# Unequal token halves of 512 and 520, branch A's gated product kept in SBUF, and later column sums in a one-core decoder layer

## The chip, the cores and the metric

The kernel runs on one core of one Trainium2 chip. The metric is the time of one execution in device microseconds (us). Work runs on five engines side by side: TensorE (PE, with its weight loads as PEld), VectorE (DVE), ScalarE (ACT), GpSimd (POOL) and SyncE (SP, which issues most of the DMAs).

## What is computed

One layer of a hybrid decoder trunk, for a prompt of 1024 tokens and 8 single-token samples, 1024 features, all in float32:

```python
xn = _rmsnorm(h, pre_g)
proj = jnp.einsum('bld,de->ble', xn, w_in)          # 1024 -> 7 * 1024
u, v, z_a, x_b, z_b, g_a, g_b = jnp.split(proj, SPLITS, axis=-1)
u = jax.nn.gelu(u)
vn = _layernorm(jax.nn.gelu(v), ln_g, ln_b)
y_a = u * _chunk_spatial_mix(vn, w_s, b_s) * jax.nn.silu(z_a)
pooled, new_pool = _pool_branch(x_b, prev_pool, pos0, w_pool, pool_scale)
y_b = pooled * jax.nn.silu(z_b)
m = (jax.nn.sigmoid(g_a) * jnp.einsum('ble,ed->bld', y_a, w_pa)
     + jax.nn.sigmoid(g_b) * jnp.einsum('ble,ed->bld', y_b, w_pb))
h = h + _rmsnorm(jnp.einsum('bld,de->ble', m, w_out), post_g)
e = jnp.einsum('blp,pd->bld', p, w_ple)
gate = jax.nn.sigmoid(jnp.einsum('bld,de->ble', _rmsnorm(h, ple_in_g), w_pg))
h = h + _rmsnorm(gate * e, ple_out_g)
```

Eleven of these products are 1024 x 1024 matrices on 1032 tokens: the seven parts of `w_in`, `w_pa`, `w_pb`, `w_out` and `w_pg`.

## The kernel before

**Tokens and halves.** Prompt and samples stand side by side as 1032 token columns (`T`). They are cut into two halves of 516 (`HT`), and a half of 516 is written by two matmuls of 258 columns (`QT`), one into each of the two 512-word banks of a PSUM buffer.

**Float32 through two parts.** Every operand is split into a high part (a rounded copy, made by ACT) and a low part (the rest, made by DVE): `split`. A product is then three: high x high, high x low, low x high. So `product` runs, for 4 blocks of 128 features, 3 pairs of parts and 2 pieces, 24 matmuls of 258 columns.

**Strassen.** A "pass" multiplies 256 output features (a pair of 128-blocks) by all tokens. `strassen` does it with seven products P1 to P7 of half-size blocks instead of eight, with sums of weights (S1 to S4) and of operands (T1 to T4):

```python
plan = (("P1", "A11", "B11", "r1"), ("P6", "S2", "T2", "r2"), ("P2", "A12", "B21", "r1"),
        ("P7", "S3", "T3", "r3"), ("P5", "S1", "T1", "r4"), ("P4", "A22", "T4", "r3"),
        ("P3", "S4", "B22", "r4"))
```

Each row is a product, its weights, its operand and its PSUM buffer. Two products on one buffer accumulate: P2 on P1, P4 on P7, P3 on P5, and the earlier one has to be read (`evacuate`) before the later one starts. P1 is copied by ACT into a slot `u`; P6 and P7 are added to it by DVE (`u`, `u7`); P2, P5, P4 and P3 give the four quarters of the output, by way of `user.direct` or `user.summed`. Only three PSUM buffers of this kind exist (`accp`), and they go round.

**Stages, in this order.** v (its first pair with eight plain products, `classical`), ga, u and za by turns, xb and zb by turns with the small pooling products (`mixes`), gb: these multiply parts of `w_in` by x, four passes each. Then pa (`Merge`) and pb (`MergeB`) multiply y_A and y_B, read back from DRAM. These 35 passes and the first v pair are of the form `Features`: weights are stationary, token columns move. The last two stages, out and gate, are of the form `Tokens`: tokens are stationary, and 512 weight columns move, so that a product is 12 matmuls of 512 columns.

**Branch A's gated product.** In the pa stage `Merge` multiplies by sigmoid(g_A) (reloaded from DRAM as `ga`) and writes the result to a DRAM tensor `m1`. In the pb stage `MergeB` reloads it (the trace calls the tile `m`) and adds branch B's product into `big`, a tile of 8 x 1032 words per partition that held x, then v and pooling scratch before.

**Column sums.** The operand sums T1 to T4 of w_out and w_pg are made ahead by `column_sums`: for each of four row blocks, two loads of 512 KB, four DVE operations, two stores. `column_steps` hangs them on steps of the v stage (w_out) and of the u and za stages (w_pg).

**Who sets the order.** The kernel hands all instructions to a `Planner`, which gives each a cost and a latest start (`late`) and makes the order of every engine from them: the operation that can start soonest goes first, and among those the one due soonest. An operation may start at most `LEAD` (14 us) before it is due, a load into a slot at most `LOAD` (17 us). The 46 slots of SBUF go round too. An operation's weights are prepared (`prepare`) 3 steps ahead and fetched 6 steps ahead. So the order in the code is a wish; products may be swapped where one isn't ready. All instructions are issued on line 287, so the trace is read by tile names: `xB11h` is the high part of B11 of x, `uw` the weights of u, `acc` and `acct` the PSUM buffers of the two forms, `accm` that of the pooling mixes.

## Time and profile before

| | |
|---|---|
| time of 3 runs, median (lowest to highest) | 1029.76 us (1029.33 to 1029.83) |
| profiled execution, its span | 1029.87 us, 1028.1 us |
| mean granted TensorE clock | 0.992 |
| HBM read, written | 116.72 MB, 51.77 MB |

The span runs from the first to the last instruction; the execution's time has 1.8 us more around it. In the rows of the profile a group shows line, engine, operation, out<-in by the program's names, partitions x elements and type, the count, then busy time, mean ns of one, and the idle time before it with what ended it. "a <- b" in the waits means that a waited for b.

### The profile page before, as it was taken

The numbers are of one execution on the slowest core, as the hardware profiler recorded it, in microseconds if no ns is written. First come the engines' busy times: TensorE is split into PE (matmuls) and PEld (weight loads), VectorE is DVE, ScalarE is ACT, GpSimd is POOL, SyncE is SP. The second block draws the span as 40 slices with busy tenths as digits, with TensorE's granted clock in tenths as the row PEclk, the third lists the DMA queues.
The fourth block names the chain that finished last, engine by engine and source line by source line (L and its number), as shares of the span: only waits on it lengthen the run. The fifth ranks groups of instructions, "written<-read, shape, count | busy, mean of one in ns | idle before, by whom it ended". The sixth has DMA issues, their size and how long they took to land. (4 is left out here: it accounts for less than half of the span.)

```text
span 1028.1 us, 18781 instructions
## 1 busy us (share of the span) xinstructions
PE 1010.2 (98%) x7556; PEld 966.9 (94%) x7556; DVE 801.7 (78%) x1239; ACT 490.1 (48%) x885; POOL 76.8 (7%) x128
## 2 busy tenths in 40 slices
PE   8999999999999999999999999999999999999996
PEld 6999999999999999999999989999999998887875
DVE  5886547987678788776777887598689898879796
ACT  7764355555434333232423333472352274778563
POOL 2200000000000000000010100000000001322122
PEclk9999998999999999999999999999999999999998
DMA  9332423722254534612304066876695572488436
GB/s 337 115 124 100 167 84 102 248 84 83 83 192 158 205 141 147 217 63 73 120 16 159 24 217 231 288 271 201 191 350 195 178 286 62 105 249 304 125 80 210
DMA packets 85108, 169.25 MB, mean 165 GB/s; under 512 B 6402, under 2 KB 46386, under 8 KB 85013
## 3 DMA queue, kind: packets, MB, share of 16 engines
q1 hardware_dynamic: 82653, 160.14, 44.6%
q0 software_dynamic: 2048, 7.37, 3.9%
q8 instruction: 59, 0.97, 0.4%
q10 hardware_dynamic: 320, 0.54, 0.2%
q14 instruction: 28, 0.23, 0.1%
HBM read 116.72 MB, written 51.77 MB: 164 GB/s over the span
## 5 line engine op out<-in xcount | busy, mean ns | idle before, releaser
L287 DVE TENSOR_TENSOR u<-acc,u 128x516 f32<-128x516 f32 x106 | 73.5, 693 | 57.6 <-PE acc L287 55.2
L287 POOL TENSOR_TENSOR rstd<-ms,mhalf 128x1 f32<-128x1 f32 (+2 forms) x45 | 41.6, 927 | 231.3 <-DVE ms L287 208.4
L287 ACT ACTIVATE u<-acc 128x516 f32<-128x516 f32 x39 | 23.4, 601 | 67.2 <-PE acc L287 63.2
L287 ACT ACTIVATE zbw<-zbs 128x512 fp32r<-128x512 f32 x16 | 9.7, 628 | 34.7 <-DVE zbs L287 31.1
L287 POOL COPY big<-xb 128x1 f32<-128x1 f32 x8 | 2.9, 367 | 291.1 <-ACT xb L287 237.6
L287 ACT ACTIVATE paw<-pas 128x512 fp32r<-128x512 f32 x16 | 9.8, 629 | 30.4 <-DVE pas L287 23.7
L287 DVE TENSOR_TENSOR big<-big 128x1032 f32<-128x1032 f32 (+3 forms) x20 | 23.7, 1222 | 0.0
L287 PE MATMUL accm<-qh,wpoolw 128*128 128x258 f32 x128 | 22.0, 285 | 1.7 <-DVE zb L287 1.7
L287 ACT ACTIVATE big<-mix 128x256 f32<-128x256 f32 x32 | 12.1, 382 | 22.1 <-PE mix L287 18.5
L287 ACT ACTIVATE junk<-h 128x512 bf16<-128x512 f32 (+1 forms) x20 | 16.3, 815 | 11.6 <-DVE h L287 9.7
L287 ACT ACTIVATE pbw<-pbs 128x512 fp32r<-128x512 f32 x16 | 9.9, 628 | 25.1 <-DVE pbs L287 23.3
L287 DVE TENSOR_TENSOR big<-mix,big 128x256 f32<-128x256 f32 x32 | 13.1, 421 | 10.1 <-ACT big L287 9.8
L287 POOL MEMSET mst<- 128x1024 f32 x1 | 1.0, 956 | 263.9 <-PE acct L287 263.9
L287 ACT ACTIVATE big<-vt 128x256 f32<-128x256 f32 x32 | 12.0, 381 | 17.6 <-PE vt L287 17.5
L287 PEld LDWEIGHTS accm<-qh,wpoolw 128*128 128x128 f32 x128 | 18.1, 189 | 2.2 <-DVE zb L287 2.1
L287 ACT ACTIVATE big<-pht,gvec 128x128 f32<-128x128 f32 x64 | 17.9, 396 | 4.2 <-PE pht L287 4.2
L287 ACT ACTIVATE zaw<-zas 128x512 fp32r<-128x512 f32 x16 | 9.9, 630 | 20.4 <-DVE zas L287 12.3
L287 DVE SCALAR_TENSOR_TENSOR zb<-accm,gvec,zb 128x516 f32<-128x516 f32 x16 | 12.0, 752 | 8.7 <-PE accm L287 8.4
L287 ACT ACTIVATE gbw<-gbs 128x512 fp32r<-128x512 f32 x16 | 9.7, 626 | 17.4 <-DVE gbs L287 13.3
L287 ACT ACTIVATE uw<-us 128x512 fp32r<-128x512 f32 x16 | 9.8, 627 | 16.3 <-DVE us L287 16.0
L287 ACT ACT_TABLE_LOAD x13 | 16.7, 1283 | 1.2 <-PEq L1651 0.8
L287 PE MATMUL mix<-wst,vh 128*128 128x256 f32 x64 | 16.3, 329 | 0.9 <-DVE big L287 0.9
(686 smaller groups left out, 3763.2 us busy)
## 6 DMA issues: line engine op xcount, KB each, us to landing
ga<-ga SPq DMA_DIRECT2D x16, 516.0 KB
gb<-gb SPq DMA_DIRECT2D x16, 516.0 KB
ya<-za SPq DMA_DIRECT2D x8, 516.0 KB
yb<-zb SPq DMA_DIRECT2D x8, 516.0 KB
m<-ga SPq DMA_DIRECT2D x8, 516.0 KB
m<-m SPq DMA_DIRECT2D x8, 516.0 KB
x<-in_x_prompt_dram SPq DMA_DIRECT2D x8, 512.0 KB
vraw<-in_w_in_dram SPq DMA_DIRECT2D x8, 512.0 KB
```

The source lines that it names most:

```text
L287: getattr(getattr(self.nc, e), method)(*args, **kwargs)
```

## The change

- The token halves are 512 and 520 (`HALF`, `WIDE`). The operands B11, B21 and T4 are narrow: one matmul of 512 columns writes a whole bank. The other four are wide: two of 260. Sums of a narrow and a wide operand take the missing 8 columns as zero, so T2's last 8 columns are those of T3, and `u` has its last 8 set to zero by POOL (`memset`).
- P4 has its own PSUM buffer r5 and stands ahead of P5; T4 is loaded and cut ahead of T1.
- `Merge` writes branch A's gated product into `big`, and `MergeB` adds to it there; `m1` is gone. Three of y_A's operands are loaded through free rows of `big` instead of slots.
- The column sums of w_out and w_pg hang on steps 8 to 46 of the u and za stages. The stores of the sums of y_A and y_B are four DMAs a block instead of two.
- `LOAD` is 14 us; a slot counts as taken by whichever of its users comes first; a memset has a cost of its own; scratch outputs of squares go to slots, and `junk` is half as wide. The prompt's tokens 512 to 515 are not loaded a second time.

```diff
-HT = T // 2
-QT = HT // 2
 HALF = 512
...
+WIDE = T - HALF
+QT = WIDE // 2
...
-    LOAD, LEAD, PATIENCE, RATE, SPARE = 17.0, 14.0, 60.0, 0.36, 3
+    LOAD, LEAD, PATIENCE, RATE, SPARE = 14.0, 14.0, 60.0, 0.36, 3
...
+        @staticmethod
+        def pieces(ps, wide):
+            if not wide:
+                return [(ps[:, 0, :HALF], slice(0, HALF))]
+            return [(ps[:, q, :QT], slice(q * QT, (q + 1) * QT)) for q in range(2)]
...
+        wide = what not in ("B11", "B21", "T4")
         for k in range(4):
-            (wh, wl), (xh, xl) = weights, operand(k)
+            (wh, wl), (xh, xl) = weights, operand.at(what, k)
             for i, (w, x) in enumerate(((wh, xh), (wh, xl), (wl, xh))):
-                for o, c in form.pieces(ps):
+                for o, c in form.pieces(ps, wide):
...
-                ("P7", "S3", "T3", "r3"), ("P5", "S1", "T1", "r4"), ("P4", "A22", "T4", "r3"),
+                ("P7", "S3", "T3", "r3"), ("P4", "A22", "T4", "r5"), ("P5", "S1", "T1", "r4"),
                 ("P3", "S4", "B22", "r4"))
...
+                both = slot("u", form.sums)
+                at["u"], at["u7"] = both[:, 0], both[:, 1]
+                if form.tail:
+                    nc.gpsimd.memset(at["u"][:, HALF:], 0.0)
+                nc.scalar.activation(out=at["u"][:, :HALF], in_=ps, func=AF.Copy)
...
             elif p == "P4":
-                user.summed(1, 0, ps, at["u"], at["u7"])
+                user.summed(1, 0, ps, at["u7"][:, :HALF])
...
+                if what == "T2":
+                    split(quarter(kk, 0), hi[:, :, :HALF], lo[:, :, :HALF])
+                    split(quarter(2 + kk, 1)[:, :, HALF:], hi[:, :, HALF:], lo[:, :, HALF:])
...
+            dma(r[:, :HALF], lo[:, :HALF])
+            dma(r[:, HALF:w], hi[:, 2 * HALF :])
+            dma(r[:, w:], lo[:, HALF:])
         spill(key + "high", b, hi)
...
+        def row(self, m, j):
+            return halves(big[:, 2 * self.pair + m, :], j)
+
         def direct(self, m, j, ps):
-            o = halves(self.out[m], j)
+            mul(self.row(m, j), ps, halves(self.out[m], j))
...
+    class MergeB(Merge):
...
+            o, row = halves(self.out[m], j), self.row(m, j)
             mul(o, ps, o)
-            self.merge(m, j)
...
+            add(row, row, o)
...
-    PARTS = ("B11", "T2", "B21", "T3", "T1", "T4", "B22")
+    PARTS = ("B11", "T2", "B21", "T3", "T4", "T1", "B22")
...
-    column_steps("wo", w_out, [(vsteps[1][5], vsteps[2][1]), (vsteps[2][2], vsteps[2][5]),
-                               (vsteps[2][6], vsteps[3][2]), (vsteps[3][3], vsteps[3][6])])
-    column_steps("wg", w_pg, [(uflow[16 + 5 * i], uflow[19 + 5 * i]) for i in range(4)])
+    for n, (key, src) in enumerate((("wo", w_out), ("wg", w_pg))):
+        column_steps(key, src, [(uflow[8 + 5 * (4 * n + i)], uflow[11 + 5 * (4 * n + i)]) for i in range(4)])
...
-    LAST = ("P1", "P6", "P7", "P5", "P4", "P3", "P2")
+    LAST = ("P1", "P6", "P7", "P4", "P5", "P3", "P2")
```

More of the change, by code (lines that the diff above doesn't have):

```diff
@@ L182, in wanted @@
                 live.append(name)
-        for name, users in self.users.items():
-            if self.tags.get(name) == "slot":
-                next(iter(users)).fresh += 1
         for op in self.ops:
             op.waits = len(op.before)
+            op.fresh = {n for n in op.names if self.tags.get(n) == "slot"}
             for o in op.before:
@@ L405, in hybrid_step, with __init__, new @@
                     "T1": (0, 1), "T2": (0, 0), "T3": (1, 1), "T4": (1, 0)}
-        def __init__(self, name, quarter=quarter, width=HT):
-            self.name, self.quarter, self.width, self.parts = name, quarter, width, {}
+        def __init__(self, name, wide=WIDE):
+            self.name, self.wide, self.parts = name, wide, {}
+        def new(self, what, kk):
+            w = HALF if what in ("B11", "B21", "T4") else self.wide
+            self.parts[what, kk] = [slot(f"{self.name}{what}{c}", (P, 2, w), F32R) for c in "hl"]
+            return self.parts[what, kk]
         def cut(self, what):
@@ L541, in quarter, with product @@
             return big[:, 4 * k : 4 * k + 4, t * P : (t + 1) * P]
-    def product(form, ps, weights, operand, first, last, again=False):
+    def product(form, ps, weights, operand, what, first, last, again=False):
         plan.apart()
+        wide = what not in ("B11", "B21", "T4")
         for k in range(4):
-            (wh, wl), (xh, xl) = weights, operand(k)
+            (wh, wl), (xh, xl) = weights, operand.at(what, k)
             for i, (w, x) in enumerate(((wh, xh), (wh, xl), (wl, xh))):
-                for o, c in form.pieces(ps):
+                for o, c in form.pieces(ps, wide):
                     nc.tensor.matmul(o, w[:, k, :], x[:, c],
@@ L627, in run @@
                     at[r] = form.new()
-                product(form, at[r], weights.ready[a], lambda k: operand.at(b, k), new, True, not new)
+                product(form, at[r], weights.ready[a], operand, b, new, True, not new)
             def run_halves(a=a, b=b, r=r):
                 for c in (slice(0, QUART), slice(QUART, HALF)):
-                    product(columns(c), at[r], weights.ready[a], lambda k: operand.at(b, k), False, True, True)
+                    product(columns(c), at[r], weights.ready[a], operand, b, False, True, True)
                     user.direct(0, 0, at[r][:, c], c)
@@ L859, in ln_stats @@
                                 op0=ALU.mult, op1=ALU.mult)
-        lnv[t] = nm, rstd([square_sum(v[:n], n, part[:n])], n)
+        vh = lnv["cut", t] = slot("vh", (P, D), F32R)
+        lnv[t] = nm, rstd([square_sum(v[:n], n, part[:n], vh)], n)
     def ln_apply(t, n=P):
@@ L1136, in loads, with summed, direct @@
             self.out = [reload(self.key, 2 * self.pair + m, self.key) for m in range(2)]
+        def row(self, m, j):
+            return halves(big[:, 2 * self.pair + m, :], j)
         def direct(self, m, j, ps):
[L1139 to L1164 removed]
+            mul(self.row(m, j), ps, halves(self.out[m], j))
+        def summed(self, m, j, ps, u, free=None):
+            free = ps if free is None else free
+            add(free, ps, u)
+            self.direct(m, j, free)
+    class MergeB(Merge):
+        def direct(self, m, j, ps):
+            o, row = halves(self.out[m], j), self.row(m, j)
+            mul(o, ps, o)
+            add(row, row, o)
     def pairs_of(c0, cls, key):
@@ L1188, in hybrid_step @@
     gbsteps = [strassen(w, xop, u) for w, u in pairs_of(GB0, Gate, "gb")]
-    yaop, ybop = stored("ya", kept["ya"], HT), stored("yb", kept["yb"], HT)
+    flat, c = big.rearrange("p b t -> p (b t)"), [T + 4 * w for w in (0, HALF, HALF + WIDE, HALF + 2 * WIDE)]
+    through = {what: flat[:, c[i] : c[i + 1]] for i, what in enumerate(("T4", "T1", "B22"))}
+    yaop, ybop = stored("ya", kept["ya"], WIDE, through), stored("yb", kept["yb"], WIDE)
     merged = lambda src, i: src[:, 2 * i * P : (2 * i + 2) * P]
@@ L1466, in hybrid_step @@
     l, c = pbsteps[3], outsteps[0]
-    turn_over(woop, l, [*l[2:], c[0], c[1]], ("B11", "T3", "T2", "B21", "T1", "T4", "B22"))
+    turn_over(woop, l, [*l[2:], c[0], c[1]], ("B11", "T3", "T2", "B21", "T4", "T1", "B22"))
     l, c = outsteps[3], gatesteps[0]
```

220 lines of the change are left out of this document (101 added, 119 removed).

## The prediction

> **What bounds the kernel now.** I read the page first, then the busy time by stage, then the timeline of TensorE alone, then the waits.
>
> ```profile
> span 1028.1 us, 18781 instructions
> PE 1010.2 (98%) x7556; PEld 966.9 (94%) x7556; DVE 801.7 (78%) x1239; ACT 490.1 (48%) x885; POOL 76.8 (7%) x128
> ...
> PE   8999999999999999999999999999999999999996
> ...
> PEclk9999998999999999999999999999999999999998
> ```
>
> ```profile
> 237.00:400.00 163.00, 163.00 (x1357) 162.97 (x1356) 125.50 (x193) 71.58 (x111) 0.55 (x1) 1.00 0.44 153
> 690.00:840.00 150.00, 148.96 (x1229) 148.23 (x1229) 128.07 (x184) 57.37 (x80) 0.00 (x0) 1.00 0.68 237
> 840.00:930.00 90.00, 90.00 (x415) 73.28 (x414) 76.12 (x119) 61.37 (x135) 20.15 (x23) 1.00 0.52 151
> ```
>
> TensorE is busy in every slice, and from 237 to 400 us (u and za) for all of 163.00 us; the columns after the length are PE, PEld, DVE, ACT, POOL, granted clock, DMA share and GB/s. The chain that ended last covers only the last 2 us and says nothing of the middle. So a stage lasts as long as its matmuls take from start to start, plus the few waits. "Busy" is not yet "at its peak", hence the cost of one matmul has to come from starts.
>
> ```profile
> 363.07 0.41 PE L287 MATMUL acc<-xB11h,uw 128*128 128x258 f32 x2
> ...
> 383.33 0.40 PE L287 MATMUL acc<-xB11h,zaw 128*128 128x258 f32 x2
> ...
> 839.22 0.39 PE L287 MATMUL acct<-woB11h,mw 128*128 128x512 f32 x1
> ...
> 858.73 0.39 PE L287 MATMUL acct<-woB11h,mw 128*128 128x512 f32 x1
> ```
>
> ```profile
> 363.07:383.33 20.26, 20.26 (x170) 20.26 (x169) 18.39 (x27) 7.77 (x11) 0.00 (x0) 1.00 0.30 112
> 839.22:858.73 19.51, 19.51 (x86) 15.78 (x85) 19.25 (x26) 11.64 (x20) 0.96 (x1) 1.00 0.18 70
> ```
>
> Here is one whole Strassen pass of each form, from its first product to the first of the next (the count of a window takes in two matmuls that reach over its edge). A feature pass is 7 products of 24 matmuls of 258 columns: 20.26 us / 168 = 120.6 ns each. A token pass is 7 products of 12 matmuls of 512: 19.51 us / 84 = 232.3 ns. Two matmuls of 258 cost 241.2 ns, one of 512 costs 232.3. The slope between the two sizes is (232.3 - 120.6) / 254 = 0.44 ns a column, so about 7 ns of a matmul do not depend on its width.
>
> **The change, part by part.**
>
> *Merged matmuls.* A feature pass keeps four wide products (24 matmuls, now of 260 columns) and has three narrow ones (B11, B21, T4) of 12 matmuls of 512. There are 35 such passes (3 for v, 4 each for ga, u, za, xb, zb, gb, pa, pb). That merges 35 x 36 = 1260 pairs; the first v pair, which takes eight plain products, merges 4 x 12 = 48 and the four pooling mixes another 48. 1356 pairs x 8.9 ns = 12.1 us less. The wide ones, 35 x 96 + 96 + 96 = 3552, each get two columns more: 0.88 ns, 3.1 us more. No row shows 260 columns; nothing below the 258 row is likely, and twice the slope would be 6.2 us, so the bounds are 0 and 6.2, and I take 3.1, the 258 row being two columns away. **Net -9.0 us**, all of it on the engine that sets the end. The form 128x512 into these accumulators is what the token passes run already.
>
> The Trainium skill speaks against this size: "TensorE: Matmul & The Clock Gate", section "Wait — 56ns, not 53.3ns?", gives a warm matmul as columns over 2.4 GHz plus a fixed 2.5 ns or so. By that, an estimate, a merged pair would save 4.2 ns, a wide matmul would cost 0.83 ns more, and the sum would be -2.7 us. The two passes above differ from it: they leave about 7 ns that are fixed and 0.44 ns a column, and I go by them.
>
> *The accumulator of P4, and the order P4, P5, P3.* P4 now has its own PSUM buffer and no longer waits for P7's evacuation. But P3 accumulates on P5's buffer and now follows it directly, and P5 has to be read first. What stands in between is up to the planner, which on TensorE takes whatever can start soonest: the next pass's P1, whose operands are cut and whose weights are prepared three steps ahead. It does this already where something is late:
>
> ```profile
> 692.84 0.28 PE L287 MATMUL acc<-yaB11h,paw 128*128 128x258 f32 x1
> ...
> 695.74 0.41 PE L287 MATMUL acc<-yaB22h,paw 128*128 128x258 f32 x2
> ```
>
> There the next pass's B11 ran before this pass's B22. With P1 (2.8 us) in the gap, the evacuation is covered:
>
> ```profile
> L287 DVE TENSOR_TENSOR u<-acc,u 128x516 f32<-128x516 f32 x106 | 73.5, 693 | 57.6 <-PE acc L287 55.2
> L287 POOL MEMSET mask<- 128x8 f32 x4 | 0.4, 103 | 0.0
> L287 DVE TENSOR_TENSOR big<-pxe,gvec 128x16 f32<-128x16 f32 x4 | 0.6, 164 | 0.0
> L287 ACT ACTIVATE sst<-smixs 128x64 fp32r<-128x64 f32 x1 | 0.3, 257 | 0.0
> ```
>
> I cost it at 0. Without that cover it is the price of a rival below. P6 of the next pass then waits for P4's buffer, three products old, P4 for P6's buffer, two products old: no tighter than now, where P4 waits for P7's reading with one product between.
>
> *Small instructions.* 35 memsets of 128x8 on POOL (0.10 us each, 3.6 us on an engine that is 7% busy). Behind each stands the addition of P6, one product or 2.9 us later; a memset queued behind one of POOL's own waits would delay it, and with it P4's buffer. The tail of T2 adds 4 ACT and 4 DVE operations (0.26 and 0.16 us), and four DVE ones of that size go from the start. Scratch in a slot instead of `junk` changes no duration. All 0, in idle time of DVE (78% busy) and ACT (48%).
>
> *Branch A's product stays in `big`.* The multiplications and additions on DVE are as many as before; what goes is DMA.
>
> ```profile
> L287 SPq DMA_DIRECT2D m<-ga x8: 319/381/743, 701.2 to 784.1; - x8
> L287 SPq DMA_DIRECT2D m<-m x8: 382/418/3173, 757.9 to 821.3; - x8
> ```
>
> 16 transfers of 516 KB, 8.3 MB of the 150 us x 237 GB/s = 35.6 MB moved from 690 to 840 us, and the 3.2 us for which SP stood in one reload (the three numbers are ns: least, median, most). That stage has a TensorE wait that ends with a late weight (total us, times, longest):
>
> ```profile
> PE accm L287 <- DVE zb L287: 1.7, 2, 1.4
> PE acct L287 <- ACT ge L287: 1.0, 2, 0.5
> PE mix L287 <- DVE big L287: 0.9, 1, 0.9
> PE acc L287 <- ACT pbw L287: 0.9, 1, 0.9
> PE acct L287 <- DVE ms L287: 0.5, 1, 0.5
> ...
> ACT pbw L287 <- DMA pbraw<-in_w_pb_dram: 2.5, 1, 2.5
> ```
>
> `pbraw` landed late, then ACT, then TensorE. Against it stands the lead of loads, cut from 17 to 14 us. I take **-1.0 us** (bounds: -2 if a second short wait goes too, 0 if the shorter lead gives it back). Sixteen more store DMAs, eight of them 8 columns wide, go out where the sums of ya and yb are stored; they are read back only in the pa and pb stages.
>
> *Column sums made later.* Sixteen additions of 0.69 us for each of w_out and w_pg, 11.0 us of DVE, and their 8 loads and 8 stores of 512 KB each. Those of w_out leave the v and ga stages for u and za, those of w_pg move 12 steps back. From 237 to 400 us DVE is busy for 125.50 of 163.00; with 11 more it is at 84%. Cost 0 while DVE keeps the rest; if it did not, an evacuation late by an operation shows as a TensorE wait of about 0.7 us.
>
> *Stalls that are re-dealt.* The planner makes a new order, so every one-off stall is drawn again. The largest is here:
>
> ```profile
> 163.81 0.60 ACT L287 ACTIVATE u<-acc 128x516 f32<-128x516 f32 x1 [3.89 <-PE smix L287]
> ...
> 165.71 0.58 PE L287 MATMUL mix<-wst,vh 128*128 128x256 f32 x1 [0.88 <-DVE big L287]
> ...
> 166.63 0.52 PE L287 MATMUL acc<-xT2h,gaw 128*128 128x258 f32 x1
> ...
> 171.90 0.38 PE L287 MATMUL mix<-wst,vh 128*128 128x256 f32 x1
> ```
>
> ACT sat until `smix` was done (a slot that changed hands), the mix waited for it 0.9 us, and just then the granted clock fell: the T2 product took 5.27 us where 2.89 is usual. About 4 us in all with the slow mixes around it. It may stay or go; the sum holds it as it is (bounds -4 and 0).
>
> *The end.* The last pass now runs P4, P5, P3 and P2 in two halves. Its last half waits today for ACT:
>
> ```profile
> 1018.44 0.28 PE L287 MATMUL acct<-wgB21h,hw 128*128 128x256 f32 x1
> 1018.76 0.38 ACT L287 ACTIVATE ge<-acct 128x256 f32<-128x256 f32 x1 [0.41 <-PE acct L287]
> 1019.19 0.39 PE L287 MATMUL acct<-wgB21h,hw 128*128 128x256 f32 x1 [0.47 <-ACT ge L287]
> ```
>
> With P5's reading outstanding, P2's first half can go before P3 and P3 between the halves: the 0.6 us go, and P3's longer chain (add, sigmoid, two multiplications, square) ends about as much nearer to the end. 0, between -0.6 and +1.5.
>
> **Sum**: -9.0 - 1.0 = -10.0 us. The profiled execution took 1029.87 us (span 1028.1 and 1.8 around it), 0.1 over the median 1029.76 of the runs, so **1019.8 us**.
>
> **The rivals.**
>
> *P3 waits for P5 (slower).* If the planner leaves P3 right behind P5, TensorE idles while DVE reads P5. The rows of the end give the price of such a hand-over: 0.75 us between two matmul starts where 0.12 is usual, for an evacuation of 0.38; with 0.69 it is 0.63 + 0.31 = 0.94 us. 43 passes x 0.94 = 40 us, hence 1029.87 - 10.0 + 40.4 = 1060. It decides from 11 uncovered passes on, where 10.3 us eat the gain. For it: the order in the code itself has nothing between them. Against it: the swap in the pa stage, and the few waits of TensorE that the present order leaves. Chance 0.07.
>
> *The new order has more waits (no difference).* The waits listed above come to 5 us and the slow clock to 2.4 more; another order could double or triple them, above all where DVE is nearly full (19.25 of 19.51 us in the token pass above), and 8 to 12 us more give 1028 to 1032. For it: DVE's work stays while TensorE's shrinks. Against it: the one buffer shared with a single product between now occurs once in a pass, not twice, and the pb stage gets DMA to spare. Chance 0.08.
>
> *Half the merge's worth.* The token pass may owe its speed to its stage: PEld is busy 73.28 of 90.00 us there and 162.97 of 163.00 in u and za. If only half of the 8.9 ns came from merging, -6.0 + 3.1 - 1.0 gives 1026. The page's rule named above would land close to this, with its 2.5 ns fixed. Against it: both kinds of pass are at full clock, without waits, and with a weight load for every matmul. Chance 0.07. That the change doesn't do what it says is part of it: narrow products that stay in two pieces would show as 128x256 forms.
>
> *The stall at 164 us and the slow clock go too.* Another slot for `u` and no w_out sums on DVE near there: -4 more, 1016, and down to 1013 if the waits of the mixes and the gate go as well. Chance 0.28.
>
> **How the numbers follow.** The forecast, 1017 to 1025, has 0.50; the stall's end 0.28; half the worth 0.07; no difference 0.08; slower 0.07. The first three are faster by over 0.2% (2.1 us, about what a measurement of this kernel can tell from no change): 0.85. Same 0.08, slower 0.07. The range 1013 to 1026.5 leaves out the last two cases and a little of the rest; it takes in 6.2 instead of 3.1 us for the 260 columns.
>
> **What would show it.** Some 6200 matmuls instead of 7556. A feature pass from B11 to B11 of 20.02 us, narrow products of 2.79 and wide ones of 2.92. On TensorE the next pass's B11 between T1 and B22, and no wait `acc <- DVE` there. No `m` among the DMA issues, and no `pbw` wait on DMA. Wrong would be: a matmul of 260 columns above 123 ns, one of 512 above 236 ns in u and za, waits of over 10 us in all behind P5, or a second stretch of reduced clock.

## The result, and the profile after

| | before | after |
|---|---|---|
| time, median (lowest to highest) | 1029.8 us (1029.33 to 1030.72, 6 runs) | 1005.7 us (1005.36 to 1006.97, 6 runs) |
| ratio to before, 95% interval | | 0.9768 [0.9755, 0.9781] |
| profiled execution, its span | 1029.87 us, 1028.1 us | 1006.03 us, 1003.7 us |
| mean granted TensorE clock | 0.992 | 0.998 |

The kernel became 24 us faster. The forecast was 10 us, 1019.8, and its range ended at 1013: the direction was right, the size wrong by more than a factor of two. (Of before_fresh, below, one execution, the profiled one, took 1985 us; the figures for that kernel are of its other nine.)

The page of the changed kernel, its first lines and the clock:

```profile
span 1003.7 us, 16146 instructions
PE 987.7 (98%) x6200; PEld 887.4 (88%) x6200; DVE 798.0 (80%) x1237; ACT 488.1 (49%) x887; POOL 78.1 (8%) x162
...
PEclk9999999999999999999999999999999999999999
```

TensorE still sets the end, with 6200 matmuls in place of 7556, exactly the 1356 merged pairs. The stretch of reduced clock near 165 us isn't there in this execution.

One feature pass, B11 of u to B11 of za, in the timeline of TensorE (first rows of its products) and as a window (length, then PE, PEld, DVE, ACT, POOL, clock, DMA share, GB/s):

```profile
309.17 0.40 PE L289 MATMUL acc<-xB11h,uw 128*128 128x512 f32 x1
...
311.95 0.40 PE L289 MATMUL acc<-xB22h,zaw 128*128 128x260 f32 x2
...
314.83 0.40 PE L289 MATMUL acc<-xT2h,uw 128*128 128x260 f32 x2
...
326.11 0.40 PE L289 MATMUL acc<-xT1h,uw 128*128 128x260 f32 x2
...
328.99 0.39 PE L289 MATMUL acc<-xB11h,zaw 128*128 128x512 f32 x1
```

```profile
309.17:328.99 19.82, 19.82 (x135) 18.24 (x133) 17.28 (x24) 7.76 (x11) 0.10 (x1) 1.00 0.61 230
```

A narrow product takes 311.95 - 309.17 = 2.78 us, as forecast (2.79), and a wide one 314.83 - 311.95 = 2.88, where 2.92 was forecast and a product of 258 columns took 2.89. The pass is 19.82 us (forecast 20.02). At both ends B11 of the next pass stands between T1 and B22, where the forecast put it.

The waits of TensorE in the changed kernel (total us, times, longest), all of them:

```profile
PE warm L289 <- POOL ident masks.py:199: 1.9, 1, 1.9
PE acct L289 <- DVE ms L289: 1.6, 1, 1.6
PE acct L289 <- DVE hw L289: 1.2, 1, 1.2
PE e L289 <- ACT wehi L289: 1.2, 1, 1.2
PE e L289 <- DVE welo L289: 0.8, 1, 0.8
PE pst L289 <- DVE x L289: 0.2, 1, 0.2
PE smix L289 <- DVE sv L289: 0.2, 1, 0.2
```

In the stages from ga to pb no wait is left but one of 0.2 us: `accm`, `mix` and `pbw` of the list before are gone.

**Where the 24.4 us of span went.** Two sums over all matmul starts (own reckoning from the traces): the time from a product's first matmul to the next product's, as a median by kind; and the lost time, all by which a step from one start to the next exceeds its usual length (the median of its shape) by over 40 ns, which holds waits and reduced clock alike.

| term | forecast, us | measured, us |
|---|---|---|
| 113 narrow products, 2.895 to 2.781 us each | -12.1 | -12.9 |
| 148 wide products, 2.895 to 2.875 us each | +3.1 | -3.0 |
| lost time of TensorE, 23.2 to 14.2 | -1.0 | -9.0 |
| from the last matmul to the end, 7.9 to 9.2 | 0 | +1.3 |
| sum | -10.0 | -23.6 |

The remaining 0.8 us wasn't split up. Of the 23.2 us lost before, 4.4 lie in steps at reduced clock (1.6 in the start, 2.8 in ga); in the profiled execution of the changed kernel none do. Such a stretch isn't in every execution: with those of the trace the mean granted clock is 0.992, and in single executions of the kernel before it goes from 0.992 to 0.998. The 7 of 76 at 0.997 or 0.998 took 1029.5 us in the mean, the 30 at 0.993 took 1030.5. So the trace puts 4.4 us into these stretches, while the times show about 1.

### The profile page after: what moved, and what is told of

Its sections match the earlier page's. It is cut to its first block, busy times and chain, and to the rows that moved or that the text cites. A ratio compares the mean times of both kernels' runs of the same rounds, so it can differ in the third digit from the quotient of the medians.

```text
span 1003.7 us, 16146 instructions
## 1 busy us (share of the span) xinstructions
PE 987.7 (98%) x6200; PEld 887.4 (88%) x6200; DVE 798.0 (80%) x1237; ACT 488.1 (49%) x887; POOL 78.1 (8%) x162
## 5 line engine op out<-in xcount | busy, mean ns | idle before, releaser
L289 DVE TENSOR_TENSOR u<-acc,u 128x520 f32<-128x520 f32 (+1 forms) x90 | 62.5, 695 | 38.7 <-PE acc L289 34.0
L289 POOL TENSOR_TENSOR rstd<-ms,mhalf 128x1 f32<-128x1 f32 (+1 forms) x45 | 41.6, 927 | 213.8 <-DVE ms L289 191.5
L289 ACT ACTIVATE u<-acc 128x512 f32<-128x512 f32 x39 | 23.2, 595 | 36.2 <-PE acc L289 35.9
L289 DVE TENSOR_TENSOR big<-big 128x1024 f32<-128x1024 f32 (+4 forms) x20 | 23.6, 1216 | 0.0
L289 DVE TENSOR_TENSOR xb<-acc,u 128x520 f32<-128x520 f32 (+1 forms) x12 | 8.3, 694 | 19.1 <-PE acc L289 19.1
L289 PE MATMUL accm<-qh,wpoolw 128*128 128x260 f32 (+1 forms) x96 | 20.9, 319 | 0.0
L289 ACT ACTIVATE big<-mix 128x256 f32<-128x256 f32 x32 | 12.1, 383 | 17.5 <-PE mix L289 16.9
L289 DVE TENSOR_TENSOR v<-acc,u 128x520 f32<-128x520 f32 (+1 forms) x9 | 6.3, 697 | 14.9 <-PE acc L289 14.8
L289 DVE TENSOR_TENSOR acc<-acc,u 128x512 f32<-128x512 f32 (+1 forms) x16 | 11.1, 696 | 8.7 <-PE acc L289 8.7
L289 DVE SCALAR_TENSOR_TENSOR zb<-accm,gvec,zb 128x512 f32<-128x512 f32 (+1 forms) x16 | 12.0, 751 | 6.6 <-PE accm L289 6.5
L289 ACT ACTIVATE xbw<-xbs 128x512 fp32r<-128x512 f32 x16 | 9.8, 624 | 14.7 <-DVE xbs L289 12.2
```

What stands on the lines that cost most here:

```text
L289: getattr(getattr(self.nc, e), method)(*args, **kwargs)
```

## The experiments

Two things are to be explained: why wide matmuls of *more* columns became cheaper, and what took 9 us of lost time away. Each median below is to be held against the kernel before as it was measured beside it (1029.8 to 1030.5 us), which the ratio does.

| kernel | median, us | ratio to before [95%] |
|---|---|---|
| pieces_256_260 | 1020.8 | 0.9909 [0.9895, 0.9924] |
| narrow_in_two | 1016.7 | 0.9870 [0.9855, 0.9884] |
| shift2 | 1029.4 | 0.9991 [0.9982, 1.0000] |
| shift4 | 1017.9 | 0.9877 [0.9861, 0.9893] |
| m1_in_dram | 1016.6 | 0.9877 [0.9858, 0.9896] |
| old_sums | 1010.0 | 0.9804 [0.9789, 0.9820] |
| load17 | 1011.4 | 0.9817 [0.9802, 0.9833] |
| load12 | 1008.9 | 0.9791 [0.9777, 0.9806] |
| old_fresh | 1012.0 | 0.9828 [0.9809, 0.9847] |
| p5_p4_p3 | 1005.5 | 0.9761 [0.9744, 0.9779] |
| last_old | 1006.7 | 0.9768 [0.9753, 0.9782] |
| before_m1_in_big | 1028.3 | 0.9982 [0.9972, 0.9992] |
| before_sums_late | 1030.9 | 1.0007 [0.9998, 1.0017] |
| before_p4_buffer | 1046.2 | 1.0158 [1.0141, 1.0175] |
| before_fresh | 1028.6 | 0.9986 [0.9977, 0.9996] |
| before_planner | 1037.0 | 1.0066 [1.0051, 1.0081] |
| before_planner_m1 | 1030.3 | 1.0006 [0.9996, 1.0016] |
| before_planner_m1_sums | 1028.9 | 0.9992 [0.9982, 1.0001] |

A name with `before_`, and pieces_256_260, is the kernel before with an edit; the others are the changed kernel with an edit.

### What a matmul costs: width, merging, or where its operand starts

Theory: the second of two pieces of 258 columns starts 258 x 4 = 1032 bytes into a row, 8 bytes past a multiple of 16, and that costs. Rival: the gain is the merging itself, with a fixed cost of some 7 ns for each matmul.

**pieces_256_260**: the kernel before, with pieces of 256 and 260 columns in place of 258 and 258. As many matmuls and columns; the second piece starts at byte 1024.

```diff
-        pieces = staticmethod(lambda ps: [(ps[:, q, :QT], slice(q * QT, (q + 1) * QT)) for q in range(2)])
+        pieces = staticmethod(lambda ps: [(ps[:, 0, QUART:], slice(0, QUART)),
+                                          (ps[:, 1, : HT - QUART], slice(QUART, HT))])
```

> The kernel before, with halves of 516 kept, but each half written by matmuls of 256 and 260 columns instead of 258 and 258, side by side across the border of the two banks. The columns are as many, the matmuls as many, the order of work the same; only the second piece now starts 1024 bytes into its row instead of 1032. Theory 'place' (a moving operand that does not start on a multiple of 16 bytes costs some 3.5 ns more per matmul: in the trace of before the first piece takes 118.7 ns and the second 122.3, after the change 119.5 and 119.9): a feature product falls from 2.895 to about 2.85 us, 261 of them give -11.5 us, so about 1018. Theory 'width' (258 columns are slow as such, or the feature stage was slow from waits): no change beyond 3 us, 1027 to 1033. If the second piece is slow only because a new weight load follows it, its time stays near 122 ns and nothing changes.

**narrow_in_two**: the changed kernel, with each narrow product as two matmuls of 256 columns.

```diff
-                return [(ps[:, 0, :HALF], slice(0, HALF))]
+                return [(ps[:, q, :QUART], slice(q * QUART, (q + 1) * QUART)) for q in range(2)]
```

> The changed kernel with one part undone: the narrow products go as two matmuls of 256 columns, one into each bank, instead of one of 512; 1356 matmuls are added back and nothing else. The prediction's sizing (about 7 ns of a matmul do not depend on its width): 1356 x 7 = 9.6 us more, about 1015. The other sizing (aligned pieces take 118.7 ns at 258 and 231.8 at 512 columns, so about 4 ns are fixed): 5.6 us more, about 1011. A theory by which merging is worth nothing here, since the weight loads are hidden: 1006.

**shift2 and shift4**: the changed kernel with every operand that is cut into parts moved by 2 or by 4 words (8 or 16 bytes) within a slot that is longer for it; 45 slots in place of 46.

```diff
-            self.parts[what, kk] = [slot(f"{self.name}{what}{c}", (P, 2, w), F32R) for c in "hl"]
+            pair = [slot(f"{self.name}{what}{c}", (P, 1044), F32R) for c in "hl"]
+            self.parts[what, kk] = [t[:, 2 : 2 + 2 * w].rearrange("p (k t) -> p k t", k=2) for t in pair]
```

> The changed kernel with every high and low part of the strassen operands moved by 2 words (8 bytes) inside its slot, and 45 slots instead of 46 to make room. Theory 'place': both pieces of a wide product and the one piece of a narrow product of x, ya and yb (also wo and wg) now start at 8 bytes past a multiple of 16: wide matmuls go from about 119.7 to 123 ns, 3360 x 3.5 = 11.8 us more than shift4, and up to 6 us more if matmuls of 512 columns suffer as well. Theory 'width': the same as shift4 within 1.5 us.

> The control for shift2: the same layout and 45 slots, the parts moved by 4 words (16 bytes). Theory 'place' with a grain of 16 bytes: pieces as after the change, 119.5 to 120 ns, and a time of 1005.7 give or take 3 for the order that one slot less brings. If the grain is 32 bytes or more, the pieces of this kernel are slower than those of the changed kernel.

One pass of u each, as a window, in the order pieces_256_260, narrow_in_two, shift2, shift4:

```profile
359.65:379.62 19.97, 19.97 (x170) 19.97 (x169) 18.31 (x27) 7.76 (x11) 0.00 (x0) 1.00 0.31 112
```

```profile
354.30:374.28 19.98, 19.98 (x170) 19.98 (x169) 18.40 (x26) 8.59 (x13) 0.00 (x0) 1.00 0.40 142
```

```profile
334.43:354.57 20.14, 20.14 (x135) 18.52 (x133) 15.35 (x26) 9.32 (x14) 0.10 (x1) 1.00 0.64 232
```

```profile
330.99:350.85 19.86, 19.86 (x135) 18.27 (x134) 15.12 (x26) 9.31 (x14) 0.10 (x1) 1.00 0.66 237
```

The lengths are what counts. 20.26 us before falls to 19.97 with the same 168 matmuls and as many columns: the second piece starts elsewhere, and with it the cut between the pieces and the place of the first in PSUM have moved. shift2 and shift4 differ in the start alone, by 8 bytes: with the same 132 matmuls 19.86 rises to 20.14. The mean of a matmul, start to start, by piece (own reckoning from the traces; products with a step over 135 ns, or 245 ns at 512 columns, are left out):

```
kernel           columns  second piece or operand starts  ns of the matmul
before           258      first piece, byte 0             118.7
before           258      second, byte 1032               122.3
pieces_256_260   256      first, byte 0                   118.0
pieces_256_260   260      second, byte 1024               119.9
after            260      first, byte 0; second, 1040     119.6; 119.9
after            512      byte 0                          231.4
narrow_in_two    256      first, byte 0; second, 1024     117.9; 117.6
shift4           260; 512 16 bytes on                     119.9, 119.8; 231.8
shift2           260; 512 8 bytes on                      121.8, 122.3; 233.4
```

On an aligned start all sizes lie on one line: (231.4 - 117.75) / 256 = 0.444 ns a column and about 4 ns that are fixed. Eight bytes past a multiple of 16 cost 1.6 to 3.5 ns more. That a piece is the second of its pair is not the reason: where both start on a multiple of 16, in the changed kernel and in narrow_in_two, they differ by 0.3 ns. So a merged pair saves 235.5 - 231.4 = 4.1 ns by itself, over 1356 pairs 5.6 us. The second pieces' 3.5 ns, in these pairs and in the 1776 pairs of wide matmuls, are 10.9 us; the columns (four fewer a narrow pair, four more a wide one) come to +0.8. Together -15.7, the measured -15.9. The theory holds and the rival gets a third: **two thirds of the matmul gain are the 16-byte start, one third is the merging.** The times agree: pieces_256_260 gains 9.4 us over the kernel before as measured beside it, where its piece times give 9.6 (11.5 were expected); shift2 is 11.5 us behind shift4 by the medians and 8.4 by the profiled executions, where the piece times give 10.8. narrow_in_two is 11.0 us behind the changed kernel, of which 5.6 are the pairs and the other half lost time that the order brings (19.8 us in all, 14.2 in the changed kernel). Its time alone, 1016.7, would fit the 7 ns of the prediction (1015 expected) better than the 4 ns (1011); the lengths of its matmuls decide. In pieces_256_260 the lost time stays at 24.0 us, though every product became shorter. shift4 was expected within 3 us of the changed kernel and is 12 behind, with 6.7 us more lost time in the xb and zb stages. The one slot less, in this kernel with longer slots for the parts, is the likely price; the two weren't separated.

### Who took the lost time away: parts undone

Theory: the in-SBUF product, the later sums and the planner's edits each free slots or DMA, and each carries a share. Rivals: P4's buffer and the order P4 before P5, or mere luck of a new order. The lost time by stage (us, own reckoning from starts):

```
                        start    v    ga  u/za xb/zb   gb    pa    pb  gate   all
before                    6.7  2.0   5.2   0.4   0.4  3.1   0.0   1.9   2.9  23.2
after                     5.8  1.7   1.6   0.3   0.3  0.1   0.0   0.0   3.8  14.2
m1_in_dram                5.7  1.7   1.6   0.3   0.3  0.1   0.0  11.0   3.8  25.1
old_sums                  5.3  1.7   4.2   0.3   0.3  0.1   0.0   0.0   3.8  16.3
load17                    5.7  1.7   1.7   0.3   1.6  1.2   0.0   0.4   5.2  18.4
load12                    5.5  1.7   1.8   0.6   1.3  0.1   1.2   0.1   4.4  17.1
old_fresh                 5.5  1.7   1.5   3.1   0.9  2.7   0.0   0.0   3.3  19.2
p5_p4_p3                  5.7  2.0   1.2   0.3   0.4  0.0   0.0   0.2   4.9  15.3
last_old                  7.2  1.7   1.6   0.3   0.3  0.1   0.0   0.0   4.5  16.3
```

**m1_in_dram**: the changed kernel, `Merge` writes to DRAM and `MergeB` reloads, as before.

```diff
         def direct(self, m, j, ps):
-            mul(self.row(m, j), ps, halves(self.out[m], j))
+            o = halves(self.out[m], j)
+            mul(o, ps, o)
+        def store(self):
+            for m, t in enumerate(self.out):
+                spill("m1", 2 * self.pair + m, t)
...
+            self.others = [reload("m1", 2 * self.pair + m, "m1") for m in range(2)]
...
-            add(row, row, o)
+            add(self.row(m, j), o, halves(self.others[m], j))
```

> The changed kernel with branch A's gated product written to DRAM and reloaded again (8.3 MB of DMA, 16 slots' worth of reloads back). Theory 'DMA' of the prediction: the pb stage waits for late weights again, 1 to 2 us, about 1007. Rival: the waits in pb belonged to the old order or the old buffers, and nothing changes (1006).

TensorE's wait in it, then DVE's timeline around that place, and windows of it:

```profile
PE acc L289 <- DVE ybT4l L289: 6.8, 1, 6.8
```

```profile
747.58 0.68 DVE L289 TENSOR_TENSOR big<-gb,m 128x512 f32<-128x512 f32 x1
...
752.76 1.22 DVE L289 TENSOR_TENSOR ybT4l<-ybT,ybT4h 128x1024 fp32r<-128x1024 f32 x1 [4.50 <-DMA m<-ga]
```

```profile
745.00:750.00 5.00, 2.27 (x13) 1.62 (x11) 3.26 (x6) 0.20 (x1) 0.00 (x0) 1.00 1.03 415
750.00:755.00 5.00, 0.96 (x2) 0.83 (x3) 2.24 (x2) 1.67 (x3) 0.00 (x0) 0.75 0.14 55
755.00:760.00 5.00, 5.00 (x24) 4.65 (x23) 4.71 (x6) 0.63 (x1) 0.10 (x1) 0.57 0.00 0
```

The low part of T4 needed a slot that a store of `m1` (`m<-ga`) still read, while the DMA engines were full (share 1.03). DVE stood 4.50 us for it, TensorE 6.8 us behind it, and the matmuls after that ran at a clock of 0.57. So the product in SBUF is worth 10.8 us here, by way of a slot that a transfer holds. One or two had been expected.

**old_sums**: the column sums at their old places.

```diff
-    for n, (key, src) in enumerate((("wo", w_out), ("wg", w_pg))):
-        column_steps(key, src, [(uflow[8 + 5 * (4 * n + i)], uflow[11 + 5 * (4 * n + i)]) for i in range(4)])
+    column_steps("wo", w_out, [(vsteps[1][5], vsteps[2][1]), (vsteps[2][2], vsteps[2][5]),
+                               (vsteps[2][6], vsteps[3][2]), (vsteps[3][3], vsteps[3][6])])
+    column_steps("wg", w_pg, [(uflow[16 + 5 * i], uflow[19 + 5 * i]) for i in range(4)])
```

> The changed kernel with the column sums of w_out and w_pg back on their old steps in the v, ga and u stages. Theory 'sums': DVE's 11 us in v and ga are what made the ga stage wait; 3 to 4 us come back there, about 1009, and the granted clock may drop near 165 us again. Rival 'slots': the ga stall was a slot that changed hands; then ga stays near 1.6 us of gaps and the time near 1006.

The time is 4.2 us longer. Two waits come back in the ga stage, whose lost time rises from 1.6 to 4.2 us, all of it without reduced clock; 0.6 us more pass behind the last matmul. That is what the profiled execution shows, which is 3.0 us slower than that of the changed kernel.

```profile
PE mix L289 <- DVE big L289: 1.2, 1, 1.2
...
PE acc L289 <- ACT gaw L289: 0.7, 1, 0.7
```

**load17 and load12**: the first number of `SPARE = 14.0, 14.0, ...`, the lead of loads `LOAD`, is 17 or 12.

> The changed kernel with loads allowed 17 us ahead of their due time again instead of 14. If the shorter lead frees slots that the ga and gb stages need, gaps come back there: 1008 to 1010. If the lead only moves loads, 1006, within 2 us. If 14 is too short somewhere (the prediction counted that as a possible loss), it is faster: 1003 to 1005.

> The changed kernel with loads allowed only 12 us ahead instead of 14. 17 had cost 5.7 us by slots that were taken too early (waits in xb/zb, gb and gate). If fewer slots held is still worth something: 1003 to 1005, in the gate stage, where 3.7 us of gaps are left. If 12 is too short for a load of 512 KB, weights come late: 1007 or more, with waits that end with a DMA.

14 us is the best of the three, by 5.7 and 3.2 us. With 17 lost time comes back in xb and zb, gb and gate, but not in ga, where it had been expected too; with 12 it is in xb and zb, pa and gate, and none of TensorE's waits there ends with a DMA.

**old_fresh**: a slot counts as taken by its first user in the code's order, as before, not by whichever comes first.

```diff
-            op.fresh = {n for n in op.names if self.tags.get(n) == "slot"}
+        for name, users in self.users.items():
+            if self.tags.get(name) == "slot":
+                next(iter(users)).fresh += 1
...
-            for name in list(o.fresh):
-                for user in self.users[name]:
-                    user.fresh.discard(name)
```

> The changed kernel with the old accounting of slots (the first user in the code counts). Matmuls as in the changed kernel. Theory (the accounting is what took the waits of ga and gb away): 2 to 6 us of waits come back, gb among them with 1 to 3, time 1008 to 1012. Rival (it hardly matters): within 1 us of the changed kernel's 1005.7.

6.3 us are lost, 2.8 of them in u and za, 2.6 in gb, where waits of the pooling mixes are there again:

```profile
PE accm L288 <- DVE zb L288: 0.8, 2, 0.4
PE accm L288 <- ACT wpoolw L288: 0.8, 1, 0.8
```

**p5_p4_p3 and last_old**: the old order P5, P4, P3 everywhere, P4 keeping r5 (in the pa and pb stages P5's sum then overwrites the values to which P4 is added, so one quarter of those products is computed from another value); and the old order in the last pass alone.

```diff
-                ("P7", "S3", "T3", "r3"), ("P4", "A22", "T4", "r5"), ("P5", "S1", "T1", "r4"),
+                ("P7", "S3", "T3", "r3"), ("P5", "S1", "T1", "r4"), ("P4", "A22", "T4", "r5"),
...
```

```diff
-    LAST = ("P1", "P6", "P7", "P4", "P5", "P3", "P2")
+    LAST = ("P1", "P6", "P7", "P5", "P4", "P3", "P2")
```

> The changed kernel with one thing undone: the products stand in the old order P5, P4, P3 again (T1 loaded and cut before T4), with P4's own buffer kept. Theory 'order': the waits that went from TensorE (9 us less in gaps: 3.6 in ga, 3.0 at the last pooling mixes in gb, 1.9 in pb) went because P4 is early and only P5 to P3 is tight, a place the next pass fills; then some 3 to 6 us of gaps come back, 1009 to 1012. Theory 'the buffer alone': 1006, gaps as in the changed kernel. The rival of the prediction, by which P5 right before P3 costs: this kernel is faster than the changed one.

> The changed kernel with the last pass of the gate stage alone back in the order P5, P4, P3, P2. With P3 behind P5 the last pass ends in P2, P3, P2, and the time from the last matmul to the end is 9.2 us where it was 7.9 before. Expected: the end falls by 1.2 us, TensorE waits 0.6 us between P2's halves as before, in all 0.5 to 1 us less than the changed kernel: about 1005.

Neither moves the time by more than 1 us, so in the changed kernel the order of the products is out as a rival. P4's own buffer stays in both runs: what it does in the changed kernel wasn't tried. last_old had been expected 0.5 to 1 us faster and is 1 us slower; its profiled execution has a stretch of half clock in the start (10.7 to 14.1 us), that of the changed kernel none.

Undone one at a time, the in-SBUF product, the later sums, the shorter lead and the accounting of slots cost 10.8, 4.2, 5.7 and 6.3 us. That is 27 us, where 9.0 us of lost time went in all: the parts hang on each other.

### The parts alone, in the kernel before

If each part had its own worth, it would show in the kernel before as well.

**before_m1_in_big** has the in-SBUF product alone, **before_sums_late** the later sums alone (the diff of old_sums turned round).

```diff
         def direct(self, m, j, ps):
-            o = halves(self.out[m], j)
-            mul(o, ps, o)
-            self.merge(m, j)
+            mul(self.row(m, j), ps, halves(self.out[m], j))
```

> The kernel before with one part of the change alone: branch A's gated product stays in the tile big, no writes to m1 and no reloads of it. The changed kernel without this part was 10.8 us slower, all of it in the pb stage, where a slot was held by a write to m1. Theory 'slots and queue': in the kernel before, the only waits of the pb stage are 1.9 us of gaps; these go, so 1028, and no more. Theory 'worth by itself': about 10 us less, 1020.

> The kernel before with the later column sums alone. In the changed kernel the old place cost 2.9 us in the ga stage (gaps 1.6 to 4.2). Theory 'sums': ga loses some 3 us, and with the wait the stretch of half clock at 165 us (2.4 us) may go as well: 1025 to 1027. Rival 'slots': the new order brings other waits and the time stays within 2 us of 1029.8.

The first gains 1.75 us, as the theory of slots had it. The second gains nothing that can be told, and its trace keeps the stretch of half clock at 165 us. What was worth 10.8 and 4.2 us in the changed kernel is worth next to nothing in the old one.

**before_p4_buffer** has P4's buffer and the order P4, P5, P3 alone.

```diff
-                ("P7", "S3", "T3", "r3"), ("P5", "S1", "T1", "r4"), ("P4", "A22", "T4", "r3"),
+                ("P7", "S3", "T3", "r3"), ("P4", "A22", "T4", "r5"), ("P5", "S1", "T1", "r4"),
```

> The kernel before with one edit of the change alone: P4 gets a PSUM buffer of its own, r5, and stands ahead of P5, T4 ahead of T1; the pieces stay 258 wide, all else as before. Its matmuls are as many and as wide, so a pass keeps its 20.26 us. Theory (the third buffer's turn is what held the pooling mixes of the gb stage): TensorE's idle time in gb falls from 3.1 us to under 0.5 and the time to about 1027, ratio 0.997. Rival (those waits hang on slots and on when loads start, as one slot less and the 17 us lead each brought 1.2 us of them back): gb keeps about 3 us, time 1029 to 1031, ratio 1.000. A third case: P4 and P5 both outstanding ahead of P3 adds waits elsewhere, over 1032.

It is 16 us slower, beyond the 1032 of the third case. TensorE's lost time in ga is 15.8 us in place of 5.2; some 5 us more are lost in the gate stage, and the end is 1.3 us longer. The two longest waits of TensorE, both in ga, then DVE's timeline in that stage, and windows of it:

```profile
PE acc L287 <- ACT gaw L287: 2.9, 1, 2.9
PE mix L287 <- DVE vl L287: 2.6, 1, 2.6
```

```profile
188.03 0.69 DVE L287 TENSOR_TENSOR woraw<-woraw,woraw 128x512 f32<-128x512 f32 x1 [0.30 <-DMA woraw<-in_w_out_dram]
188.76 0.69 DVE L287 TENSOR_TENSOR woraw<-woraw 128x512 f32<-128x512 f32 x1
189.49 1.42 DVE L287 TENSOR_TENSOR woraw<-woraw,woraw 128x512 f32<-128x512 f32 x2
190.82 1.22 DVE L287 TENSOR_TENSOR vl<-big,vh 128x1024 fp32r<-128x1024 f32 x1
```

```profile
190.00:192.00 2.00, 0.00 (x0) 0.00 (x0) 1.97 (x3) 0.49 (x2) 0.00 (x0) 0.87 1.10 392
192.00:194.00 2.00, 1.91 (x9) 1.91 (x10) 1.83 (x5) 0.56 (x2) 0.00 (x0) 0.50 1.02 405
194.00:196.00 2.00, 2.00 (x11) 2.00 (x11) 0.52 (x1) 0.00 (x0) 0.00 (x0) 0.50 1.03 420
```

DVE makes four additions of the column sums of w_out, 2.8 us, ahead of `vl`, the low part of v, for which TensorE waits 2.56 us (to 192.09); then the clock is at half until 198. The wait for the weights `gaw` ends at 202.62, again with additions of these sums on DVE ahead of it, and the clock is at half until 208.6. Whether later sums would have ended these two waits wasn't tried; the two that old_sums brings back in ga are likewise a mix's for DVE and a product's for `gaw`. In gb 2.1 of the 3.1 us stay. The waits are not at P3 behind P5, of which the third case spoke.

**before_fresh** has the new accounting of slots alone, **before_planner** that and the lead of 14 us; **before_planner_m1** adds the in-SBUF product, **before_planner_m1_sums** the later sums too. All four keep the 7556 matmuls. (The diffs are those of old_fresh, load17, m1_in_dram and old_sums turned round.)

> The kernel before with the planner's new accounting of slots alone (a slot counts as taken by whichever of its users comes first). Matmuls as before, so stages keep their length but for waits. Theory (the accounting sets when slots change hands, and the pooling mixes of gb wait for slots): the 3.1 us of waits in gb fall under 0.5 and the 5.2 of ga by a microsecond or more, time 1023 to 1027. Rival (the accounting re-deals waits but takes none away; the sum of all parts is needed): 1028 to 1034, waits of 20 us or more in all.

> The kernel before with the new accounting of slots and the lead of loads of 14 instead of 17 us. Theory (the planner's edits carry the 9 us of waits that went, since the 17 us in the changed kernel brought 4.2 us of waits back): waits 14 to 18 us in all, time 1019 to 1025. Rival (they need the slots that m1's removal and the later sums set free): waits stay above 20 us, time 1027 to 1034.

> The kernel before with the planner's edits (accounting of slots, lead of loads 14 us) and with branch A's gated product kept in SBUF, nothing else: as many matmuls of 258 columns as before. Theory (the planner's edits take the waits of gb and part of those of ga away, and the reloads and stores of m1 are what made them cost 5.7 us in pa and 6.9 in pb): gb stays under 0.5 us of waits, ga near 3, pa and pb fall back to under 1 each, all waits 15 to 19 us, time 1021 to 1026. Rival (the waits of pa and pb come from the shorter lead itself): pa and pb keep 8 us or more, time 1032 to 1038. A third case: gains that do not add, 1027 to 1031.

> The same with the later column sums as well. Theory (the sums made later free slots and DVE in ga, worth 4.2 us in the changed kernel): ga falls from about 3 to under 2 us of waits, time 1 to 3 us under the run without them, 1019 to 1024. Rival (the parts re-deal waits, and their sum is not to be had from a list): no better than the run without them, or worse.

```
                        start    v    ga  u/za xb/zb   gb    pa    pb  gate   all
before                    6.7  2.0   5.2   0.4   0.4  3.1   0.0   1.9   2.9  23.2
before_planner            6.7  2.0   3.2   0.3   0.4  0.0   5.7   6.9   4.4  30.1
before_planner_m1         6.8  2.0   3.2   0.3   0.4  0.0   5.7   0.0   4.3  23.3
before_planner_m1_sums    6.7  2.0   1.2   0.3   0.4  0.0   6.5   0.0   4.4  22.1
```

(before_fresh gains 1.5 us by its times and isn't in this table.) Here most parts take away one thing, and put another in its place. The planner's edits end the waits of gb, and bring 5.7 us into pa and 6.9 into pb; the kernel is 7 us slower. The in-SBUF product ends those of pb and leaves those of pa as they are. The later sums make the kernel 1.4 us faster by the medians. In ga the column shows mostly the clock (own reckoning): 2.8 us at reduced clock in the kernel before, 1.5 in before_planner and before_planner_m1, none in before_planner_m1_sums; the waits there are 1.0, 0.5, 0.6 and 0.0 us. The waits of before_planner, and of before_planner_m1:

```profile
PE acc L288 <- DVE ybT4l L288: 3.2, 1, 3.2
PE acc L288 <- DVE yaB22l L288: 2.4, 1, 2.4
...
PE acc L288 <- DVE paw L288: 1.2, 1, 1.2
...
PE acc L288 <- DVE pbw L288: 1.1, 1, 1.1
```

```profile
PE acc L288 <- DVE yaB22l L288: 2.4, 1, 2.4
...
PE acc L288 <- DVE paw L288: 1.2, 1, 1.2
```

So both theories of before_planner_m1 were half right: pb's waits were those of `m1`, pa's were not. What is left in pa is the low part of y_A's B22, cut too late. DVE's and TensorE's timelines of before_planner_m1, then of the changed kernel:

```profile
687.77 0.40 PE L288 MATMUL acc<-yaB22h,paw 128*128 128x258 f32 x2
689.32 2.37 DVE L288 TENSOR_TENSOR yaB22l<-yaB,yaB22h 128x1032 fp32r<-128x1032 f32 x2
690.60 0.51 PE L288 MATMUL acc<-yaB22l,paw 128*128 128x258 f32 x2 [2.42 <-DVE yaB22l L288]
```

```profile
665.90 1.23 DVE L289 TENSOR_TENSOR yaB22l<-big,yaB22h 128x1040 fp32r<-128x1040 f32 x1
...
668.26 1.23 DVE L289 TENSOR_TENSOR yaB22l<-big,yaB22h 128x1040 fp32r<-128x1040 f32 x1
...
674.21 0.40 PE L289 MATMUL acc<-yaB22h,paw 128*128 128x260 f32 x2
```

The first matmul of pa stands at 670.45 in the one and at 651.65 in the other. From there on the two cuts start after 18.9 us in before_planner_m1, and after 14.3 and 16.6 in the changed kernel. The product that needs them starts after 17.3 and after 22.6 us, because in the changed kernel gb's last product and the next pass's B11 run ahead of it. So two things differ: the cut is earlier, from a row of `big` in place of a slot (the three operands of y_A that are loaded through free rows), and the product is later. Which of the two empties pa wasn't tried, nor were P4's buffer in the changed kernel and the scratch outputs in slots undone by themselves.

## Why the prediction was wrong, point by point

- **What bounds the kernel.** Right. TensorE sets the end before and after, and a stage lasts as long as its matmuls and waits: every gain above is one or the other.
- **Merged matmuls, 12.1 us.** The size came out (12.9), the reason did not. "So about 7 ns of a matmul do not depend on its width" is the step that failed: the 120.6 ns of that pass are the mean of 118.8 for first and 122.4 for second pieces, and the second holds the price of a start 8 bytes past a multiple of 16. The size came out all the same, because it was the difference of two measured rows, whatever made it. The fixed part is 4 ns, and merging alone gives 4.1 ns a pair. The rival "half the merge's worth" had that right and was still further off in time, since it kept the +3.1. The Trainium skill's rule, "TensorE: Matmul & The Clock Gate", section "Wait — 56ns, not 53.3ns?", with 2.5 ns fixed, is nearer to these 4 ns than the 7 were; its 0.417 ns a column (an estimate from its 2.4 GHz) is not what these traces show, 0.444.
- **Wide matmuls.** "The wide ones, 35 x 96 + 96 + 96 = 3552, each get two columns more: 0.88 ns, 3.1 us more": the term with the wrong sign, -3.0 us. "Nothing below the 258 row is likely" closed the range on the side where the answer lay. Halves of 520 make the second piece start at byte 1040, a multiple of 16. What was overlooked was to be seen in the trace of before: with the products' matmuls set apart by piece, first and second differ by 3.5 ns.
- **The order P4, P5, P3.** Right: the next pass's P1 fills the gap, and with the old order, P4 keeping its buffer, the time is the same to 0.2 us. The rival in which P3 waits for P5 (1060) did not come. That buffer and order alone cost 16 us in the kernel before was not foreseen; most of it is in ga.
- **Branch A's product in `big`, -1.0 us.** Mis-sized. In the finished kernel pb lost 1.9 us of waits, the upper bound; but without it the changed kernel is 10.8 us slower, since the other edits put 11 us of lost time into pb that this one takes out. Its worth was reckoned in bytes moved; what TensorE waited for was a slot that such a transfer held.
- **Column sums later, 0.** Mis-sized: 4.2 us in the changed kernel, of which 2.6 are lost time in ga. Cost was weighed where the sums go; the gain lies where they left. In the kernel before the same edit gains nothing.
- **Stalls that are re-dealt, 0 (-4 to 0).** This term failed: but for branch A's 1.0 us the lost time was held as it was, and it fell by 9.0. The rival with 0.28 came nearer, but stopped at 1013: ga -3.6, gb -3.0, pb -1.9 and start -0.9 us, against gate +0.9. In gb and pb it was no lottery: the planner's edits and the in-SBUF product switch these waits on and off, in both kernels. In ga the later sums do so plainly in the changed kernel alone; 2.8 of the 3.6 us there, and all that the start gained, are stretches of reduced clock, which come in one execution and not in the next.
- **The end, 0 (-0.6 to +1.5).** +1.3, within its bounds; with the old order in the last pass it is 8.0 us again, and the kernel is no faster: in that trace start and gate lose 2.1 us more, the start by its stretch of half clock.

The steps that failed, then, are these two. A matmul's cost was taken to hang on its width alone, with one price for both pieces and 7 ns of it fixed; that left out what the second piece's start costs, and gave the wide term the wrong sign (6.1 us). And the lost time was held as it was (8 us, waits and reduced clock together).

## What to carry to other kernels

Before a cost is split into a fixed and a width part, set the matmuls apart by where their operand starts; a piece length that is a multiple of 4 words made each second piece about 3.5 ns cheaper than its width lets expect, at no other price that these runs show. In a kernel whose order a planner makes from a scarce pool of slots, the worth of a part can't be read from the kernel before: the same edit gave 1.7 us there and 10.8 in company, and P4's buffer with the new order cost 16 us alone, while going back to the old order in company changed nothing. So ask of each edit which slots, and until when, it holds, and try the parts undone from the end as well as done from the start.

## What the runs showed of the hardware

A moving operand in the fp32r form that starts 8 bytes past a multiple of 16 costs a matmul of 260 columns 1.9 to 2.5 ns (shift2 against shift4), one of 512 columns 1.6 ns; a second piece of 258 columns costs 3.5 ns more than the first (kernel before). How it is at 4 bytes wasn't measured.

After the longer waits of TensorE the granted clock was 0.50, in stretches of 3.4 or 6.8 us that reached 3 to 7 us beyond the wait: in before_p4_buffer after 2.56 us (the windows above), in load17 after 2.61, in before_planner_m1_sums after 2.42, in m1_in_dram after 6.8. Such a wait costs its length and about half of the time behind it again: the 6.8 and 0.9 us of waits in pb of m1_in_dram became 11.0 us of lost time. A wait of 2.19 us in the gate stage of before_p4_buffer left the clock at 1.00. The Trainium skill, "TensorE: Matmul & The Clock Gate", section "What's actually happening", has the clock halved after an idle window of about 3.4 us; the half clock is what these traces show, but 2.42 to 2.61 us without work were enough.

Length alone does not decide it. In the ga stage 16 matmuls of 8x8 take 1.9 us (`smix`), and in 8 of the 19 traces, the one of before among them, the clock fell 2 to 5 us after they began; in the other 11, with the same 16 matmuls, it did not. In before_planner it fell with no wait ahead of it. TensorE's timeline there, and windows of it:

```profile
161.78 1.95 PE L288 MATMUL smix<-diag,sv 8*128 8x8 f32 x16
```

```profile
161.00:163.00 2.00, 2.00 (x18) 1.86 (x17) 1.33 (x3) 0.63 (x1) 0.00 (x0) 1.00 0.67 268
163.00:165.00 2.00, 2.00 (x14) 1.98 (x14) 0.90 (x7) 0.54 (x1) 0.55 (x1) 0.72 0.94 291
165.00:167.00 2.00, 2.00 (x11) 2.00 (x11) 1.80 (x4) 1.71 (x4) 0.96 (x1) 0.50 0.69 244
```

So the 0.88 us wait of the kernel before, ahead of the T2 product that then took 5.27 us, isn't needed for the reduced clock there. Why it fell in some traces and not in others stays open.
